# Block sums of the down projection's weights loaded into their own place, and output rows with buffers of their own, in a one-core encoder layer

## The chip, the cores and the metric

The kernel runs on one core of a Trainium2 chip (trn2). The metric is the device time of one execution in microseconds (us), the median over several runs. The profiled execution is one run of its own; its trace has a span (first instruction to last) a little shorter than its time.

## The reference

One layer of an encoder over 512 positions of 1024 features, all in float32: a norm, a combined projection, gated spatial mixing beside dilated window attention, a merge, and then a feed-forward block. The change lies in the last two lines of it:

```python
n2 = rms_norm(h, norm_mlp_pre[l])
hid = jnp.square(jax.nn.relu(jnp.einsum('bsd,df->bsf', n2, w_up[l])))     # 512 x 4096
mlp_out = jnp.einsum('bsf,fd->bsd', hid, w_down[l])                       # 512 x 1024
h = h + rms_norm(mlp_out, norm_mlp_post[l])
```

## The kernel before

**Products in three parts.** TensorE (PE) multiplies float32 values as pairs: `split_into` (L78 to L80) has ScalarE (ACT) write the high part and VectorE (DVE) write the low part, source minus high part. A product is three matmuls, high by high, high by low, low by high (`acc3`, L1026 to L1030). A split weight piece is called `hl` and has 5 buffers; a split piece of the hidden activations is called `hhl`. One split is 128x1024 elements on ACT and as many on DVE.

**The up projection** (loop at L970) runs in 14 rounds. The last round's results leave the accumulators by ACT L983, L986, L988 and DVE L984, L990, L992, L993, and last of all by DVE L998, after which ACT applies Relu (L1000) and Square (L1001). L998 is the last reader of one accumulator bank.

**The down projection** sums over 4096 hidden features, that is 32 tiles of 128. The first 16 tiles are done in eight plain steps (`plain`, two tiles each, 48 matmuls of 128x512). The other 16 are done as two chunks `c` of a 2-by-2 block scheme with seven products of block sums in place of eight (Winograd's form): `first_sums` forms b22 - b12 into `tsum[c]` and sums of the hidden blocks into `a21` and `s2`; later steps add b11 to `tsum`, subtract it from b22, and subtract it from b21. Weight loads go through a tag `raw` with two buffers of 1 MB (names `dnw`), issued by SyncE's queue (SP). A load waits until both what the buffer held is split or summed, and SP waits in order, so a load that has to wait holds the ones behind it.

**The order.** Each engine takes its instructions strictly in the order in which the scheduler of the language left them; the scheduler places an instruction by its own estimate of when it is ready. In that order three plain steps come first, then `first_sums(0)`, plain step 3, `first_sums(1)`, plain step 4, and the products of the block sums with three more plain steps between. Loads of `first_sums` use the same two `raw` buffers: b22 and b12 of a chunk fill both, and the next plain step's weights wait until the two subtractions (L1079) have read them.

**The end.** The last 24 matmuls finish output rows 0 and 1 (tiles of 128 positions); rows 2 and 3 were finished by the 24 before. `finish` (L1139) loads the residual `h2` for the row (queue of GpSimd, POOL), squares the row on ACT with its output as junk into `o` (L1154), multiplies by the gain on DVE (L1155, `y`), forms the norm's factor (DVE L93, then POOL L96), writes `o` (L1149, two halves) and sends it out (L1151, two DMAs of 256 KB from SP). `o` has two buffers (`lpool`), so row 0 takes the buffer of row 2 and row 1 that of row 3.

**Buffers.** `n2pool` has 8 places of 512 KB under the tag `n2`. In the up projection they hold the moving operand of the matmuls; afterwards they take `gain3`, `s2` (two), `v`, `t1` (four), and `h2` (four). `tsum` has 2 MB of its own (`sumpool`).

Of the kernel before, what the change touches and what calls it, by code (L numbers as in the profile page):

```python
# [10 lines left out]
F32 = mybir.dt.float32  # L11
F32R = mybir.dt.float32r
AF = mybir.ActivationFunctionType
ALU = mybir.AluOpType
PSUM = bass.MemoryType.PSUM

P = 128
S = 512
D = 1024
# [17 lines left out]
def block_kernel(ctx: ExitStack, tc: tile.TileContext, x, norm_mix_pre, w_in, b_gate, ln_v_gain, ln_v_bias,  # L37
                 w_spatial, b_spatial, w_branch_a, w_branch_b, w_out, norm_mix_post, norm_mlp_pre, w_up,
                 w_down, norm_mlp_post, ident_c, rope_c, mask_c, perm_c, out):
    nc = tc.nc  # L40
    x, out, w_in, w_up, w_down, w_out = x[0], out[0], w_in[0], w_up[0], w_down[0], w_out[0]
    w_branch_a, w_branch_b, w_spatial = w_branch_a[0], w_branch_b[0], w_spatial[0]

    def pool(stack, name, bufs=1, space=None, side=None):
        kw = {"side": side} if side else {}
        if space is not None:
            kw["space"] = space
        return stack.enter_context(tc.tile_pool(name=name, bufs=bufs, reuse_waits="tile", **kw))
# [20 lines left out]
    def wsplit(raw, pl=None, bufs=None, tag="w", sub=None):  # L69
        pl = pl or wpool  # L70
        shape = list(raw.shape)
        hi = pl.tile(shape, F32R, name="hi", tag=tag + "hi", bufs=bufs)
        lo = pl.tile(shape, F32R, name="lo", tag=tag + "lo", bufs=bufs)
        nc.scalar.activation(hi, raw, AF.Copy)  # L74
        (sub or nc.vector).tensor_tensor(lo, raw, hi.bitcast(F32), op=ALU.subtract)  # L75
        return hi, lo
# [210 lines left out]
    def feature_tile(wh, wl, nk, mh, ml, tag="acc"):  # L287
        ps = psA.tile([P, S], F32, name="pf", tag=tag, bufs={"acc": 4, "S": 2, "T": 1, "y": 1}[tag])
        for k in range(nk):
            mm3(ps, (wh[:, k], wl[:, k]), (mh[:, k], ml[:, k]), k == 0, k == nk - 1)  # L290
        return ps
# [27 lines left out]
    for i, (vec, n) in enumerate(((b_gate, 16), (ln_v_gain, 4), (ln_v_bias, 4), (norm_mlp_pre, 8))):  # L319
        o = (0, 16, 20, 24)[i]  # L320
# [24 lines left out]
    def seven_pairs(n, weights, moving, banks, snap, two, rows, evac, after):  # L345
        tail = None
        for i in range(n):
            c2, c1 = rows(i)
            w = weights(i)
            Y, Z, X = banks()  # L350
            product(6, Y, w, moving, True)
            if tail:
                tail()
            product(1, X, w, moving, True)
            p1, z5, u2, u3 = snap("p1", two), snap("z5", 1), snap("u2", 1), snap("u3", 1)
            nc.scalar.activation(p1, X, AF.Copy)
            nc.vector.tensor_tensor(u2, Y, p1, op=ALU.add)
            product(5, Z, w, moving, True)
            nc.scalar.activation(z5, Z, AF.Copy)
            product(2, X, w, moving, False)  # L360
            evac(i, c1[:, A], X)
            product(7, Y, w, moving, False)
            nc.vector.scalar_tensor_tensor(u3, Y, -1.0, p1, op0=ALU.mult, op1=ALU.subtract)
            product(3, Z, w, moving, False)
            nc.vector.tensor_tensor(c1[:, B], Z, u2, op=ALU.add)
            nc.vector.tensor_tensor(c2[:, B], u3, z5, op=ALU.subtract)

            def tail(i=i, w=w, Y=Y, p1=p1, c2=c2):
                product(4, Y, w, moving, False)
                nc.vector.scalar_tensor_tensor(c2[:, A], Y, -1.0, p1, op0=ALU.mult, op1=ALU.subtract)  # L370
                after(i)
        tail()
# [312 lines left out]
    for g2 in range(2):  # L685
        raw = wload([KD, 2 * P], lambda r: [(r, fcols(w_in, COL_U + g2 * 2 * P, KD, 2 * P))], "uw")
        for j in range(2):
            g = 2 * g2 + j
            wh, wl = wsplit(raw[:, :, j * P:(j + 1) * P], sub=nc.gpsimd)
            ps = psA.tile([P, S], F32, name="pf", tag="acc" if g else "T", bufs=4 if g else 1)  # L690
# [74 lines left out]
    for d in range(GSTD):  # L765
        g2 = gate_rows(d - GSTD)
        raw = gate_raw(d)
        for br in range(2):
            ps = feature_tile(*wsplit(raw[:, :, 1 - br]), KD, nhn, nln)
# [11 lines left out]
    n2pool = pool(back, "n2pool", bufs=8, side="right")  # L781
# [9 lines left out]
    halves = [slice(0, 512), slice(512, 1024)]  # L791
# [171 lines left out]
    def half_bank(tag):  # L963
        return psB.tile([P, 512], F32, name="p" + tag, tag=tag, bufs=4)[:, :256]
# [5 lines left out]
    for i in range(NSTD, KF // 2):  # L970
# [6 lines left out]
        Y, Z, X = half_bank("acc"), half_bank("acc"), half_bank("tp")  # L977
# [28 lines left out]
    lpool = pool(dn, "lpool", bufs=2)  # L1006
# [4 lines left out]
    X, W, Y, Z = [[accs[t][hf] for t in ts] for ts, hf in (((0, 1), 0), ((0, 1), 1), ((2, 3), 0), ((2, 3), 1))]  # L1011
# [5 lines left out]
    def raw_down():  # L1017
        return wback.tile([P, 2, D], F32, name="dnw", tag="raw", bufs=2)
# [7 lines left out]
    def acc3(ps, a, b, start, stop):  # L1026
        (ah, al), (bh, bl) = a, b
        nc.tensor.matmul(ps, ah, bh, start=start, stop=False, skip_group_check=True)  # L1028
        nc.tensor.matmul(ps, ah, bl, start=False, stop=False, skip_group_check=True)  # L1029
        return nc.tensor.matmul(ps, al, bh, start=False, stop=stop, skip_group_check=True)  # L1030
# [12 lines left out]
    w7 = w_down[F7 * P:].rearrange("(c j h p) d -> c h p j d", p=P, h=2, j=4)  # L1043

    def block(c, h, hf):
        raw = raw_down()
        raw = raw.rearrange("p a (b d) -> p (a b) d", d=512)
        nc.sync.dma_start(raw, w7[c, h, :, :, halves[hf]])
        return raw
# [23 lines left out]
    tsum = sumpool.tile([P, N7, 512], F32, name="tsum")  # L1073
    tsum = [tsum[:, 4 * c:4 * c + 4] for c in range(2)]
    s2 = []

    def two(out, x, y, op):
        for i in range(0, 4, 2):
            nc.vector.tensor_tensor(out[:, i:i + 2], x[:, i:i + 2], y[:, i:i + 2], op=op)  # L1079

    def first_sums(c):
        b22, b12 = block(c, 1, 1), block(c, 0, 1)
        two(tsum[c], b22, b12, ALU.subtract)
        nc.vector.tensor_tensor(a21[c], a11[c], a21[c], op=ALU.subtract)
        s2.append(n2pool.tile([P, 4, 256], F32, name="s2", tag="n2"))
        nc.vector.tensor_tensor(s2[c], a22[c], a21[c], op=ALU.subtract)

    first_sums(0)
    plain(3, order)
    first_sums(1)  # L1090
    plain(4, y_first)
    keep = hida.tile([P, 8, S], F32, name="hid")
# [34 lines left out]
    for c in range(2):  # L1127
        b22 = block(c, 1, 1)
# [10 lines left out]
    def finish(t, srcs, ys, o, ss):  # L1139
        h2 = n2pool.tile([P, D], F32, name="h2", tag="n2")  # L1140
        nc.gpsimd.dma_start(h2, h2d[tsl[t]])
        for hf in (1, 0):
            if srcs[hf] is not None:
                if ys[hf] is None:
                    ys[hf] = lpool.tile([P, 512], F32, name="y")
                weigh(srcs[hf], ys[hf], o[:, halves[hf]], ss, hf)
        r = rstd_of(ss, 1.0 / D)
        for hf, hs in enumerate(halves):
            nc.vector.scalar_tensor_tensor(o[:, hs], ys[hf], r, h2[:, hs], op0=ALU.mult, op1=ALU.add)  # L1149
        for hs in halves:  # L1150
            nc.sync.dma_start(out[tsl[t], hs], o[:, hs])  # L1151
# [23 lines left out]
    for ps, (hh, hl), ws, ts in ((Y, h4, w4, (2, 3)), (X, h, w, (0, 1))):  # L1175
        for t in range(2):
            for j in range(4):
                wh, wl = ws[j // 2]
                acc3(ps[t], (hh[:, j, tsl[t]], hl[:, j, tsl[t]]), (wh[:, j % 2], wl[:, j % 2]), False, j == 3)
            o = lpool.tile([P, D], F32, name="o")  # L1180
            if ps is Y:
                nc.vector.tensor_tensor(p1[:, t], Y[t], p1[:, t], op=ALU.add)
                finish(2 + t, [p1[:, t], None], [p1[:, t], r22[:, t]], o, sums[2 + t])
            else:
                finish(t, [X[t], None], [None, r12[:, t]], o, sums[t])
# [43 lines left out]
```

## Time and profile before

| What | Value |
|---|---|
| median of 3 runs | 803.08 us (802.73 to 803.18) |
| profiled execution, its own time | 802.89 us |
| its span | 801.1 us |
| TensorE matmul busy | 782.8 us, 98% of the span |
| VectorE busy | 593.8 us, 74% |
| ScalarE busy | 442.1 us, 55% |
| GpSimd busy | 60.2 us, 8% |
| mean granted TensorE clock | 0.995 |
| last matmul begins | 790.01 us |

The page of a profile gives busy times, a picture of the span in 40 slices, the DMA queues, the chain of work that ended last, the costliest groups and the DMA issues. A timeline row reads: start, length, engine, line of the code, operation, output and input names (buffer numbers left out), shape, count, and in brackets the idle time before it with what ended it. Matmul rows overlap: their starts are what counts, some 0.227 us apart when PE never waits. A row of the waits view reads: engine and line that waited, what it waited for, us in total, times, longest. A DMA's time to landing runs from its issue to the signal that its data are there.

### The profile page before, as it was taken

Reading aid. Unit: us, or ns where it says so; the run is one execution under the profiler, and the core shown is the slowest. Engines: PE = TensorE matmul, PEld = TensorE weight load, DVE = VectorE, ACT = ScalarE, POOL = GpSimd, SP = SyncE. Lnnn points to the kernel's source line nnn. Section 1 sums busy time; section 2 is a strip of 40 time slices with the busy share of each in tenths; the row PEclk is TensorE's granted clock in tenths of the full one; section 3 lists DMA queues with packets and bytes.
Section 4 is the critical chain, followed back from the end, with each engine's and each line's share of the span. In section 5 each row is a group of like instructions: output and inputs, shape, how many; then the busy total and the mean of one; then the engine's idle time right before and its main releaser. Section 6 shows DMA issues by size and latency. Waiting matters only on the chain.

```text
span 801.1 us, 12250 instructions
## 1 busy us (share of the span) xinstructions
PE 782.8 (98%) x4869; PEld 709.8 (89%) x4869; DVE 593.8 (74%) x956; ACT 442.1 (55%) x731; POOL 60.2 (8%) x86
## 2 busy tenths in 40 slices
PE   9999999999999999999999999999999999999994
PEld 6899999998988889999988899999999887888883
DVE  6784678978654878788646479988888546896686
ACT  6351467978576454455435447666667424543551
POOL 3300100010104300000001102000000000000001
PEclk9999999999999999999999999999999999999997
DMA  9733733353615423253456222433333354143302
GB/s 310 232 122 100 203 102 106 96 142 94 190 62 135 140 79 107 79 142 95 132 184 197 93 79 66 145 106 106 106 106 123 114 206 162 64 147 131 132 1 105
DMA packets 93706, 101.01 MB, mean 126 GB/s; under 512 B 2721, under 2 KB 74433, under 8 KB 93650
## 3 DMA queue, kind: packets, MB, share of 16 engines
q1 hardware_dynamic: 83312, 79.70, 32.0%
q0 software_dynamic: 10336, 20.54, 8.4%
q8 instruction: 38, 0.62, 0.3%
q14 instruction: 18, 0.15, 0.1%
q10 hardware_dynamic: 2, 0.00, 0.0%
HBM read 90.27 MB, written 9.96 MB: 125 GB/s over the span
## 4 chain that ended last, share of the span: by engine, by line
PE 87%; DVE 5%; DMA 3%; ACT 3%; issue 1%; POOL 0%; DVEq 0%; POOLq 0%; ACTq 0%
PE pacc L961 12%; PE pg L343 9%; PE pgacc L343 6%; PE pd L1028 5%; PE pf L84 5%; PE pd L1029 5%; PE pd L1030 5%; PE pf L85 5%; PE pf L86 5%; PE ptp L961 5%; PE pv L85 4%; PE pv L86 4%; PE pv L84 4%; PE pgS L343 3%; DMA dnw<-in_w_down_dram 2%; PE pd L84 2%
## 5 line engine op out<-in xcount | busy, mean ns | idle before, releaser
L1029 PE MATMUL pd<-hl,hhl 128*128 128x512 f32 x240 | 93.3, 389 | 0.0
L1030 PE MATMUL pd<-hl,hhl 128*128 128x512 f32 x240 | 91.3, 389 | 0.0
L1028 PE MATMUL pd<-hl,hhl 128*128 128x512 f32 x240 | 88.7, 390 | 1.4 <-ACT hl L79 1.4
L961 PE MATMUL pacc<-nt,hl 128*128 128x256 f32 x504 | 66.7, 279 | 1.4 <-DVE nt L80 1.4
L961 PEld LDWEIGHTS pacc<-nt,hl 128*128 128x128 f32 x504 | 62.2, 188 | 1.6 <-DVE nt L80 1.6
L1028 PEld LDWEIGHTS pd<-hl,hhl 128*128 128x128 f32 x240 | 45.0, 188 | 11.1 <-ACT hl L79 1.9
L1030 PEld LDWEIGHTS pd<-hl,hhl 128*128 128x128 f32 x240 | 45.1, 188 | 9.3
L1029 PEld LDWEIGHTS pd<-hl,hhl 128*128 128x128 f32 x240 | 45.1, 188 | 9.3
L79 ACT ACTIVATE hl<-dnw 128x1024 fp32r<-128x1024 f32 x28 | 29.3, 1055 | 40.6 <-PE pd L1030 17.1
L80 DVE TENSOR_TENSOR hl<-dnw,hl 128x1024 fp32r<-128x1024 f32 x28 | 33.9, 1221 | 15.9 <-ACT hl L79 15.9
L961 PE MATMUL pacc<-n,hl 128*128 128x256 f32 x336 | 44.7, 279 | 0.0
L74 ACT ACTIVATE hi<-s 128x1024 fp32r<-128x1024 f32 x30 | 31.7, 1059 | 23.6 <-DVE s L330 8.3
L84 PE MATMUL pf<-nh,hi 128*128 128x512 f32 x112 | 44.6, 398 | 0.0
L85 PE MATMUL pf<-nl,hi 128*128 128x512 f32 x112 | 43.9, 392 | 0.0
L86 PE MATMUL pf<-nh,lo 128*128 128x512 f32 x112 | 43.9, 392 | 0.0
L75 DVE TENSOR_TENSOR lo<-s,hi 128x1024 fp32r<-128x1024 f32 x30 | 36.6, 1224 | 9.7 <-ACT hi L74 9.6
L961 PEld LDWEIGHTS pacc<-n,hl 128*128 128x128 f32 x336 | 41.7, 188 | 0.1
L79 ACT ACTIVATE hl<-s 128x1024 fp32r<-128x1024 f32 x28 | 29.6, 1056 | 21.8 <-DVE s L945 15.5
L80 DVE TENSOR_TENSOR hl<-s,hl 128x1024 fp32r<-128x1024 f32 x28 | 34.2, 1221 | 6.2 <-ACT hl L79 6.2
L85 PE MATMUL pv<-lo,nh 128*128 128x512 f32 x96 | 38.2, 397 | 0.0
L86 PE MATMUL pv<-hi,nl 128*128 128x512 f32 x96 | 37.8, 397 | 0.0
L84 PE MATMUL pv<-hi,nh 128*128 128x512 f32 x96 | 37.1, 395 | 0.0
(387 smaller groups left out, 2223.4 us busy)
## 6 DMA issues: line engine op xcount, KB each, us to landing
dnw<-in_w_down_dram SPq DMA_DIRECT2D x18, 1024.0 KB, 4.9
upw<-in_w_up_dram SPq DMA_DIRECT2D x16, 1024.0 KB, 5.6
qkw<-in_w_in_dram SPq DMA_DIRECT2D x24, 512.0 KB, 5.1
gw<-in_w_in_dram SPq DMA_DIRECT2D x16, 512.0 KB, 5.2
slab<-in_w_in_dram SPq DMA_DIRECT2D x6, 1024.0 KB, 9.1
wow<-in_w_out_dram SPq DMA_DIRECT2D x4, 1024.0 KB, 4.9
w0raw<-in_w_in_dram SPq DMA_DIRECT2D x4, 512.0 KB, 6.8
v0d<-v POOLq DMA_DIRECT2D x4, 512.0 KB, 4.7
```

What stands on the lines that cost most here:

```text
L74: nc.scalar.activation(hi, raw, AF.Copy)
L75: (sub or nc.vector).tensor_tensor(lo, raw, hi.bitcast(F32), op=ALU.subtract)
L79: nc.scalar.activation(hi, src, AF.Copy)
L80: return sub.tensor_tensor(lo, src, hi.bitcast(F32), op=ALU.subtract)
L84: nc.tensor.matmul(ps, ah, bh, start=start, stop=False)
L85: nc.tensor.matmul(ps, ah, bl, start=False, stop=False)
L86: return nc.tensor.matmul(ps, al, bh, start=False, stop=stop)
L343: nc.tensor.matmul(ps, a[:, j], b[:, j], start=first and not (j or i), stop=(j == KH - 1 and i == 2), skip_group_check=True)
L961: nc.tensor.matmul(ps, a[:, j], b[:, j], start=first and not (j or m), stop=(j == KH - 1 and m == 2), skip_group_check=True)
L1028: nc.tensor.matmul(ps, ah, bh, start=start, stop=False, skip_group_check=True)
L1029: nc.tensor.matmul(ps, ah, bl, start=False, stop=False, skip_group_check=True)
L1030: return nc.tensor.matmul(ps, al, bh, start=False, stop=stop, skip_group_check=True)
```

## The change

`first_sums` no longer goes through the two `raw` buffers. b12 is loaded straight into `tsum[c]` (1 MB, one DMA), b22 in two halves of 512 KB, each into a spare place of `n2pool` (tile `b22`), and each half is subtracted in place (new L1085). `two` becomes one instruction of 128x2048 elements in place of two of 128x1024; its remaining uses are the additions of b11 and the subtractions from b21. The last two rows' `o` are taken from `n2pool` (name `o2`), each with a place of its own.

```diff
     def two(out, x, y, op):
+        nc.vector.tensor_tensor(out, x, y, op=op)
+
+    def first_sums(c):
+        nc.sync.dma_start(tsum[c], w7[c, 0, :, :, halves[1]])
         for i in range(0, 4, 2):
-            nc.vector.tensor_tensor(out[:, i:i + 2], x[:, i:i + 2], y[:, i:i + 2], op=op)
-
-    def first_sums(c):
-        b22, b12 = block(c, 1, 1), block(c, 0, 1)
-        two(tsum[c], b22, b12, ALU.subtract)
+            b22 = n2pool.tile([P, 2, 512], F32, name="b22", tag="n2")
+            nc.sync.dma_start(b22, w7[c, 1, :, i:i + 2, halves[1]])
+            nc.vector.tensor_tensor(tsum[c][:, i:i + 2], b22, tsum[c][:, i:i + 2], op=ALU.subtract)
...
-            o = lpool.tile([P, D], F32, name="o")
+            o = lpool.tile([P, D], F32, name="o") if ps is Y else n2pool.tile([P, D], F32, name="o2", tag="n2")
```

The scheduler moves instructions with it. On SP's queue, from the first load for the down projection on (with `b_7075` and `b_7078` the halves of b22 for chunk 0, `b_7144` and `b_7147` those for chunk 1):

```order
-L1035 DMA dnw<-in_w_down_dram 128x2x1024 x3
-L1048 DMA dnw<-in_w_down_dram 128x4x512 x2
+L1035 DMA dnw<-in_w_down_dram 128x2x1024 x2
+L1084 DMA b_7075<-in_w_down_dram 128x2x512
 L1035 DMA dnw<-in_w_down_dram 128x2x1024
-L1048 DMA dnw<-in_w_down_dram 128x4x512 x2
-L1035 DMA dnw<-in_w_down_dram 128x2x1024
+L1084 DMA b_7078<-in_w_down_dram 128x2x512
+L1081 DMA tsum<-in_w_down_dram 128x4x512 x2
+L1084 DMA b_7144<-in_w_down_dram 128x2x512
+L1084 DMA b_7147<-in_w_down_dram 128x2x512
+L1035 DMA dnw<-in_w_down_dram 128x2x1024 x2
```

All loads of both `first_sums` now stand together, between the loads of plain step 2 and plain step 3; the loads of plain steps 3 and 4 stand behind them in a row. In the built program `b_7075` waits for PE's product 1 of the last up round, `b_7078` and with it both `tsum` loads for its product 2, `b_7144` and `b_7147` for its product 3, for these read the places that the loads fill. The load of plain step 3 waits for the last low part of plain step 1's weights, that of plain step 4 for the last one of plain step 2's.

On DVE at the end of the up projection (L998 is the last evacuation of the last up round; the `hl` ahead of it belong to plain step 1, the first one behind it to plain step 2), a piece of the difference:

```order
 L80 TENSOR_TENSOR hl<-dnw,hl 128x1024
+L1085 TENSOR_TENSOR tsum<-b_7075,tsum 128x1024
+L1085 TENSOR_TENSOR tsum<-b_7078,tsum 128x1024
 L998 SCALAR_TENSOR_TENSOR hid<-pacc,p_6800 128x256
 L80 TENSOR_TENSOR hl<-dnw,hl 128x1024
-L80 TENSOR_TENSOR hhl<-hid,hhl 128x1024 x3
-L1084 TENSOR_TENSOR hid<-hid 128x4x256
-L80 TENSOR_TENSOR hl<-dnw,hl 128x1024
-L1086 TENSOR_TENSOR s_7149<-hid 128x1024
-L1079 TENSOR_TENSOR tsum<-dnw 128x1024 x2
-L80 TENSOR_TENSOR hhl<-hid,hhl 128x1024
+L1085 TENSOR_TENSOR tsum<-b_7144,tsum 128x1024
```

The two subtractions of chunk 0 now stand ahead of L998, the first one of chunk 1 ahead of the low part of plain step 1's activations (the first of the three `hhl`), and the second one, the next `+` row but one, behind that of plain step 2's. Before, chunk 0's stood eight instructions behind L998 and chunk 1's further still.

On POOL at the end of the program, before (`h_7882`, `h_7910`, `h_7937`, `h_7965` are the residuals of rows 2, 3, 0 and 1, `rs_out` the norm's factors in the same order of rows):

```order
L1141 DMA h_7882<-h2d 128x1024
L1141 DMA h_7910<-h2d 128x1024
L1141 DMA h_7937<-h2d 128x1024
L1141 DMA h_7965<-h2d 128x1024
L96 TENSOR_TENSOR rs_out<-rs_in_7888,neghalf 128x1
L96 TENSOR_TENSOR rs_out<-rs_in_7916,neghalf 128x1
```

and now, with the rows in the same order and row 1's residual as `h_7963`:

```order
L1143 DMA h_7880<-h2d 128x1024
L1143 DMA h_7908<-h2d 128x1024
L1143 DMA h_7935<-h2d 128x1024
L96 TENSOR_TENSOR rs_out<-rs_in_7886,neghalf 128x1
L96 TENSOR_TENSOR rs_out<-rs_in_7914,neghalf 128x1
L1143 DMA h_7963<-h2d 128x1024
L96 TENSOR_TENSOR rs_out<-rs_in_7942,neghalf 128x1
```

The residual of row 1 is now loaded after the factors of rows 2 and 3, where all four loads stood ahead of all factors before. On DVE at the end, the gain products and sums of squares of rows 0 and 1 (L1157 and L93 in the new numbering) now stand one after the other ahead of both rows' outputs (L1151); before, row 0's outputs stood between them. PE's order is the same up to plain step 3; from there on it differs only in whether the high and low parts of a weight piece are used in turn or the high part first, with the same 720 matmuls of 128x512 in the down projection.

## The prediction

> **What bounds the kernel now.** I read the page first, then the busy time by stretches of the second feed-forward half.
>
> ```profile
> span 801.1 us, 12250 instructions
> PE 782.8 (98%) x4869; PEld 709.8 (89%) x4869; DVE 593.8 (74%) x956; ACT 442.1 (55%) x731; POOL 60.2 (8%) x86
> 668.00:673.00 5.00, 3.56 (x16) 2.60 (x15) 2.64 (x3) 3.73 (x4) 0.00 (x0) 1.00 0.69 266
> 673.00:785.00 112.00, 112.00 (x495) 92.72 (x495) 88.91 (x88) 55.55 (x65) 2.17 (x4) 1.00 0.27 94
> 791.00:801.00 10.00, 0.00 (x0) 0.00 (x0) 4.25 (x8) 1.38 (x4) 1.10 (x2) 0.59 0.43 162
> ```
>
> The last three rows give a stretch, its length, the busy time of PE, weight load, DVE, ACT and POOL, then granted clock, DMA share and GB/s. PE is the bound almost everywhere; in 112 us from 673 on it never rests. Only two places are to be had: a hole of 1.44 us near 669 and the 10 us behind the last matmul. A part of the change falls on each. The chain of waits says how the hole comes about (start, length, what):
>
> ```profile
> 646.43 2.37 DVE tsum L1079 x2
> 648.82 4.75 DMA dnw<-in_w_down_dram
> 657.07 4.87 DMA dnw<-in_w_down_dram
> 662.04 2.37 DVE tsum L1079 x2
> 664.43 4.82 DMA dnw<-in_w_down_dram
> 669.27 1.06 ACT hl L79
> ```
>
> No PE row stands in it: load, sum, load, sum, load follow each other through the two raw buffers, and the last load, plain step 4's, ends in PE's wait. The timeline of PE around it, with the same place one step earlier for comparison:
>
> ```profile
> 657.67 0.39 PE L1030 MATMUL pd<-hl,hhl 128*128 128x512 f32 x1
> 657.89 1.98 PE L1028 MATMUL pd<-hl,hhl 128*128 128x512 f32 x8
> 659.71 0.39 PE L1029 MATMUL pd<-hl,hhl 128*128 128x512 f32 x1
> ...
> 668.55 0.39 PE L1030 MATMUL pd<-hl,hhl 128*128 128x512 f32 x1
> 670.38 2.14 PE L1028 MATMUL pd<-hl,hhl 128*128 128x512 f32 x8 [1.44 <-ACT hl L79]
> 672.36 0.39 PE L1029 MATMUL pd<-hl,hhl 128*128 128x512 f32 x1
> ```
>
> Undisturbed, the step from one L1030 over eight matmuls to the next L1029 takes 659.71 - 657.67 = 2.04 us; here it takes 672.36 - 668.55 = 3.81. So the hole costs 1.77 us: the start is 1.60 late, and 0.17 goes in the first eight matmuls behind it.
>
> The end, from the timelines of PE, DVE, ACT and POOL:
>
> ```profile
> 790.01 0.39 PE L1030 MATMUL pd<-hl,hhl 128*128 128x512 f32 x1
> 788.08 2.74 DVE L1149 SCALAR_TENSOR_TENSOR o<-hid,rs_out,h 128x512 f32<-128x512 f32 x4 [0.39 <-POOL rs_out L96]
> 791.72 0.60 ACT L1154 ACTIVATE o<-pd 128x512 f32<-128x512 f32 x1 [4.82 <-DMA out_dram<-o]
> 792.44 0.69 DVE L1155 TENSOR_TENSOR y<-pd,gain 128x512 f32<-128x512 f32 x1 [1.62 <-ACT o L1154]
> 793.05 0.15 DVE L93 SCALAR_TENSOR_TENSOR rs_in<-ss,rs_in 128x1 f32<-128x1 f32 x1
> 793.34 0.55 POOL L96 TENSOR_TENSOR rs_out<-rs_in,neghalf 128x1 f32<-128x1 f32 x1 [4.78 <-DVE rs_in L93]
> 793.93 0.75 DVE L1149 SCALAR_TENSOR_TENSOR o<-y,rs_out,h 128x512 f32<-128x512 f32 x1 [0.73 <-POOL rs_out L96]
> 797.41 0.75 DVE L1149 SCALAR_TENSOR_TENSOR o<-hid,rs_out,h 128x512 f32<-128x512 f32 x1
> ```
>
> ACT could square row 0 as soon as its matmuls are done. It waits 4.82 us until row 2's output has left the buffer that it writes its junk into, and DVE behind it 1.62.
>
> **The sum.** The profiled execution took 802.89 us, its span 801.1; the other 1.79 stays. It lies 0.02% under the median of 803.08, so the terms are taken from 802.89.
>
> *The hole near 669 goes: -1.77.* Plain step 3's load now waits only for the last low part of plain step 1's weights, and plain step 4's for that of plain step 2's. These two rows of DVE, and a third that is needed just below:
>
> ```profile
> 629.63 1.23 DVE L80 TENSOR_TENSOR hl<-dnw,hl 128x1024 fp32r<-128x1024 f32 x1 [0.67 <-ACT hl L79]
> 640.22 1.22 DVE L80 TENSOR_TENSOR hl<-dnw,hl 128x1024 fp32r<-128x1024 f32 x1
> 676.04 1.22 DVE L80 TENSOR_TENSOR hhl<-hid,hhl 128x1024 fp32r<-128x1024 f32 x1
> ```
>
> So the loads start at some 631 and 641, the second a few us later for the subtractions that now stand ahead, and both land some 10 us or more before PE asks (657.9 and 668.8). The loads after them move up in the same way, and splits from there on wait for PE to free an `hl` buffer, as they do from 673 on today without a rest for PE; next late is then nothing until the end. The one subtraction or addition of 2048 elements in place of two of 1024 is not in the trace; two take 2.37, one should take 2.2 to 2.5, and it lies beside the same gapless PE: 0. It makes a low part of activations behind it wait 1.2 longer, covered: the split ran at 676.04, and its product stands 72 matmuls behind 670.38, at 0.227 each near 686.7.
>
> *A new wait at the start of plain step 1.* The subtractions of chunk 0 stand ahead of L998, and they wait for a load that can't start before product 2 of the last round. What stands there now:
>
> ```profile
> 625.73 0.39 ACT L988 ACTIVATE hid<-ptp 128x256 f32<-128x256 f32 x1 [3.54 <-PE ptp L961]
> 632.68 0.42 DVE L998 SCALAR_TENSOR_TENSOR hid<-pacc,p 128x256 f32<-128x256 f32 x1 [1.82 <-PE pacc L961]
> 633.65 1.04 ACT L1000 ACTIVATE hid<-hid 128x1024 f32<-128x1024 f32 x1
> 634.59 2.94 ACT L79 ACTIVATE hhl<-hid 128x1024 fp32r<-128x1024 f32 x3
> 634.77 0.39 PE L1028 MATMUL pd<-hl,hhl 128*128 128x512 f32 x1
> 636.13 0.39 PE L1028 MATMUL pd<-hl,hhl 128*128 128x512 f32 x1
> 639.76 1.98 PE L1030 MATMUL pd<-hl,hhl 128*128 128x512 f32 x8
> ```
>
> Product 2 is over by 625.7 (ACT's first row waits for it). The second half of b22 (0.5 MB) and then `tsum[0]` (1 MB) start there. How long that takes, from the SP timeline and the group of these loads:
>
> ```profile
> 649.24 8.20 SPq L1048 DMA_DIRECT2D dnw<-in_w_down_dram  x2
> DMA to landing us min/median/max: 4.7/4.9/7.1
> ```
>
> Alone, 1 MB takes 4.75 (the chain's load of 648.82, landed at 653.57). The load issued at 649.24 behind it took up to 7.1, to 656.34: 2.77 for one more MB in line. So 1.5 MB takes 4.75 + 1.39 = 6.14 and lands at 631.9; ahead of it, three loads (0.5 MB for b22, 0.5 for the gain, 1 for plain step 2) are to be through by 625.7, which leaves little room, so I take 632.2, with 631.3 and 633 as ends. The two subtractions take 2.3 until the next instruction begins, so L998 starts at 634.5 in place of 632.68 and ends at 634.95; Relu follows on ACT, 0.94 later the high part of the activations (633.65 to 634.59), and 1.11 behind its start PE can use it (669.27 to 670.38): 637.0. PE asks at 636.13. That is 0.87 late, and with the 0.17 of a restart **+1.0**; nothing if the load lands by 631.3, 1.8 if at 633. The bank that L998 frees is asked for at 634.77, 0.2 before its new end, and that wait lies within the other. Behind L998 on DVE, the first subtraction of chunk 1 needs 3 MB through: 4.75 + 2 x 2.77 = 10.3, at 636.0; the low part of the activations behind it is then written by 638.5, and PE asks at 639.76. That cover of 1.3 us is thin; beyond it PE loses one for one.
>
> One rule speaks to this term. The Trainium skill, "DMA: Bandwidth & Descriptors", section "Anatomy of one DMA", puts a transfer at about 2.0 us plus its bytes by 436 GB/s; an estimate from it for 1.5 MB is 5.6 us, a landing at 631.3, and with it a sum of 798.1. The rows are slower for 1 MB (4.75 against 4.4 by that rule), so they decide.
>
> *The end: -3.0.* With its own buffer row 0, whose last matmul stands five ahead of the last, is squared near 789.4, and row 1 once the last matmul is through at 790.4, done at 791.05. DVE is busy with rows 2 and 3 until 788.08 + 2.74 = 790.8 and becomes the limit. Then y for row 0 at 790.8, its sum 0.6 later (792.44 to 793.05) at 791.4, y for row 1 at 791.6, its sum at 792.2. A sum's factor is ready for DVE 0.88 after it (793.05 to 793.93): 792.3 and 793.1. Row 0's outputs start at 792.35 and 793.0 (0.67 each, 2.74 by four), row 1's at 793.7 and 794.4, in place of 797.41. What follows the last output stays. Spare places for `o2` cost nothing: they hold sums and splits read long before.
>
> Sum: 802.89 - 1.77 + 1.0 - 3.0 = **799.1**.
>
> **The rivals.** *No new wait:* the first `tsum` lands by 631.3. For it, half of b22 is loaded earlier and the median landing is near the minimum; against it, 1.5 MB in line after a crowded queue. 798.1.
>
> *Row 1's residual is late.* Its load now stands on POOL behind the factors of rows 2 and 3.
>
> ```profile
> 786.96 1.61 POOL L96 TENSOR_TENSOR rs_out<-rs_in,neghalf 128x1 f32<-128x1 f32 x2 [36.89 <-DVE rs_in L93]
> DMA to landing us min/median/max: 2.9/3.5/6.3
> ```
>
> The second row is the group of the `h` loads and stores. Issued at 788.57, it lands at 791.5, 792.1 or, at worst, 794.9, while four output writes leave; it is needed at 793.7. At worst the end is 1.2 later: 800.3. The same page, section "Queues, rings and completion order", says each DMA engine takes turns between queues, so the load would share with those writes and not stand behind them; no row here shows the two together.
>
> *Both `tsum` loads come in together* rather than one by one: 2.5 MB, 4.75 + 1.5 x 2.77 = 8.9, at 634.6. PE then waits 3.3 + 0.17 = 3.5: 801.6. Against it: the load of 648.82 landed as fast as one alone with another in line behind it.
>
> *Slower than before:* DVE stands on the subtraction so long that L998, Relu and all splits behind it starve PE. It decides once the first `tsum` lands later than 631.3 + 4.6 = 635.9, for then the new wait eats 1.77 + 3.0. If all that is queued shares the engines (2.5 MB, 1 MB for chunk 1's b22, 1 for plain step 3), it is 4.5 MB: 4.75 + 3.5 x 2.77 = 14.4, at 640.1, a wait of 9.0: 807.1. The same row speaks against it.
>
> *The change doesn't do what it says near 669:* another wait, of an `hl` buffer or of ACT, holds plain step 4 as long. Then 1.77 stays: 800.9. Against it: ACT began that split at 669.27, 0.02 behind the load's landing (664.43 + 4.82).
>
> **How the numbers follow.** Forecast 0.50; no new wait 0.20; late residual 0.15; both loads together 0.08; starved PE 0.03; hole stays 0.04. The low end is no new wait and 0.2 more at the end, 797.9; the high end takes in the late residual with the load landing at 633 (800.3 + 0.8), 801.1. What lies outside is the 0.11 of the cases above and a little below. The bound of 0.2%, about what a measurement of this kernel tells from no change, is 1.6 us: faster is under 801.5, slower over 804.7. Faster: all cases but starving and half of both-together, 0.93; within it 0.04; slower 0.03.
>
> **What would show it.** In the profile after: PE without a hole near 669; a wait of DVE L1085 for `tsum`'s load, then PE's L1028 waiting for ACT L79 `hhl` near 636, some 0.9 us; no ACT wait for an output DMA; y of rows 0 and 1 in a row, and the last output 3 us closer to the last matmul. Wrong: a PE wait over 2 us near 636, a wait of L1151 for the `h` load, or a hole elsewhere between 640 and 785.

## The result, and the profile after

The changed kernel takes 801.07 us (median of 11 runs, 800.79 to 802.54), the kernel before beside it 803.15; the ratio is 0.9975, with a 95% interval of 0.9967 to 0.9984. So it is faster by 2.0 us, half of the 4.0 that were forecast. Two executions are used nowhere, one of an experiment (the first profiled one of e6 below, 2764.78 us, so that e6's stretches come from a second one, e6b) and one of before beside the last experiments (1578.76 us).

The profiled execution of after took 801.01 us. The first two lines of its page:

```profile
span 799.2 us, 12243 instructions
PE 782.9 (98%) x4869; PEld 709.5 (89%) x4869; DVE 593.7 (74%) x952; ACT 442.4 (55%) x731; POOL 60.6 (8%) x86
```

PE is busy as long as before, and the span is 1.9 us shorter. To see where, I cut the end of the program into three stretches by rows that every kernel here has. **A** goes from the start of the last up product on PE (a group of twelve L961 near 631, whose result L998 reads) to the start of the last matmul, **B** from there to the start of the last pass that writes an output, **C** from there to the end of the span. PE does the same work ahead of A in all kernels; from execution to execution A's start differs by up to 1.3 us, so the stretches are compared and not the points of time. The rows of before that the prediction does not show:

```profile
631.08 1.56 PE L961 MATMUL pacc<-n,hl 128*128 128x256 f32 x12
634.55 0.39 PE L1030 MATMUL pd<-hl,hhl 128*128 128x512 f32 x1
```

and those of after, with PE's two waits between them and DVE at the end:

```profile
631.24 1.56 PE L961 MATMUL pacc<-n,hl 128*128 128x256 f32 x12
634.71 0.39 PE L1030 MATMUL pd<-hl,hhl 128*128 128x512 f32 x1
635.96 0.50 PE L1028 MATMUL pd<-hl,hhl 128*128 128x512 f32 x1 [0.87 <-DVE hid L998]
638.06 0.50 PE L1028 MATMUL pd<-hl,hhl 128*128 128x512 f32 x1 [0.45 <-ACT hhl L79]
641.83 1.98 PE L1030 MATMUL pd<-hl,hhl 128*128 128x512 f32 x8
668.00:671.00 3.00, 3.00 (x15) 2.49 (x14) 2.25 (x1) 0.00 (x0) 0.00 (x0) 1.00 0.00 0
790.29 0.39 PE L1030 MATMUL pd<-hl,hhl 128*128 128x512 f32 x1
791.02 0.69 DVE L1157 TENSOR_TENSOR y<-pd,gain 128x512 f32<-128x512 f32 x1
791.68 0.69 DVE L1157 TENSOR_TENSOR y<-pd,gain 128x512 f32<-128x512 f32 x1
794.51 0.75 DVE L1151 SCALAR_TENSOR_TENSOR o<-hid,rs_out,h 128x512 f32<-128x512 f32 x1
```

- A: 790.01 - 631.08 = 158.93 before, 790.29 - 631.24 = 159.05 after. The hole near 669 is gone (PE is busy for all of 668 to 671), and two new waits take back what it gave: from the L1030 ahead of them to the group of eight L1030 it was 639.76 - 634.55 = 5.21, now 641.83 - 634.71 = 7.12.
- B: 797.41 - 790.01 = 7.40 before, 794.51 - 790.29 = 4.22 after. This is the gain of 3.2.
- C: 801.1 - 797.41 = 3.69 before, 799.2 - 794.51 = 4.69 after. This is a loss of 1.0 that I had at nothing. (Spans are printed to 0.1 us, so each C is good to 0.05.)

With the 0.16 that A starts later, 0.12 - 3.18 + 1.00 + 0.16 = -1.90, the difference of the spans.

Why the two waits come, from the timelines of SP, DVE and ACT in after:

```profile
626.19 1.01 SPq L1081 DMA_DIRECT2D tsum<-in_w_down_dram  x2
633.21 2.36 DVE L1085 TENSOR_TENSOR tsum<-b,tsum 128x1024 f32<-128x1024 f32 x2 [2.19 <-DMA tsum<-in_w_down_dram]
635.49 0.42 DVE L998 SCALAR_TENSOR_TENSOR hid<-pacc,p 128x256 f32<-128x256 f32 x1
636.00 1.06 ACT L1000 ACTIVATE hid<-hid 128x1024 f32<-128x1024 f32 x1 [2.10 <-DVE hid L998]
636.97 2.94 ACT L79 ACTIVATE hhl<-hid 128x1024 fp32r<-128x1024 f32 x3
```

The first `tsum` block lands at 633.1, DVE subtracts for 2.3 us, and only then comes L998, which both frees a bank (PE's first wait) and feeds Relu and the split of plain step 1's activations (PE's second wait).

The prediction counted 1.5 MB up to that landing. What SP's queue moved between the issue of the second half of `b22` (625.77) and the landing (packets, MB of a million bytes, share of 16 engines):

```profile
q1 hardware_dynamic: 1165, 2.32, 88.3%
```

In this unit the half of `b22` and the first `tsum` are 1.57 MB; some 0.7 MB more had been moved by then, nearly all for loads that were issued behind them. By 631.36 the queue had moved 1.62 MB, 1.8 us ahead of the landing. For the load of 648.82 in before, from which the price was taken, 1.27 MB had been moved when its 1.05 landed, with one load behind it; here four were issued behind. So loads in line on one queue are not moved strictly one after the other. That this overlap alone makes the landing late is read from the bytes; no run tries it.

For the end, the output writes and what else is under way. First before, then after: SP's issues, the writes' time from issue to landing, and in after POOL's load of row 1's residual:

```profile
788.86 9.65 SPq L1151 DMA_DIRECT2D out_dram<-o  x8
DMA to landing us min/median/max: 2.0/2.1/2.1
```

```profile
789.14 6.48 SPq L1153 DMA_DIRECT2D out_dram<-o  x8
DMA to landing us min/median/max: 2.6/4.2/4.3
788.81 0.58 POOL L1143 DMA_DIRECT2D h<-h2d  x1
h<-h2d POOLq DMA_DIRECT2D x1, 512.0 KB, 4.5
```

The four writes of rows 2 and 3 take 4.2 to 4.3 us instead of 2.1, those of rows 0 and 1, which set the end, 2.6 to 2.7 instead of 2.0. How the engines were shared in one microsecond of that (the DMA view of after, 791.5 to 792.5; packets, MB, share of 16 engines):

```profile
q0 software_dynamic: 63, 0.26, 70.2%
q1 hardware_dynamic: 58, 0.12, 30.5%
```

q0 is the load, q1 the writes: nearly as many packets of one as of the other, and as the load's hold about 4 KB (0.26 MB in 63) and the writes' about 2 KB (0.12 in 58), two thirds of the bytes are the load's. The Trainium skill, "DMA: Bandwidth & Descriptors", section "Queues, rings and completion order", says that each DMA engine takes turns between the queues it has work for; the trace agrees with its 63 and 58 packets. In which order one engine took them it does not tell.

### The profile page after: what moved, and what is told of

Same layout as the page of the kernel before. It is cut to its first block, busy times and chain, and to the rows that moved or that the text cites. A ratio compares the mean times of both kernels' runs of the same rounds, so it can differ in the third digit from the quotient of the medians.

```text
span 799.2 us, 12243 instructions
## 1 busy us (share of the span) xinstructions
PE 782.9 (98%) x4869; PEld 709.5 (89%) x4869; DVE 593.7 (74%) x952; ACT 442.4 (55%) x731; POOL 60.6 (8%) x86
## 4 chain that ended last, share of the span: by engine, by line
PE 91%; DVE 4%; ACT 2%; DMA 1%; issue 1%; POOL 0%; DVEq 0%; SPq 0%; POOLq 0%; ACTq 0%
PE pacc L961 11%; PE pg L343 9%; PE pd L1028 6%; PE pd L1029 6%; PE pd L1030 6%; PE pgacc L343 6%; PE pf L84 5%; PE pf L85 5%; PE pf L86 5%; PE ptp L961 5%; PE pv L85 4%; PE pv L86 4%; PE pv L84 4%; PE pgS L343 3%; PE pd L84 2%; PE pd L86 2%
## 5 line engine op out<-in xcount | busy, mean ns | idle before, releaser
L1029 PE MATMUL pd<-hl,hhl 128*128 128x512 f32 x240 | 93.3, 389 | 0.0
L1028 PE MATMUL pd<-hl,hhl 128*128 128x512 f32 x240 | 91.8, 390 | 1.3 <-DVE hid L998 0.9
L1030 PE MATMUL pd<-hl,hhl 128*128 128x512 f32 x240 | 91.1, 389 | 0.0
L961 PE MATMUL pacc<-nt,hl 128*128 128x256 f32 x504 | 66.7, 279 | 1.4 <-DVE nt L80 1.4
L961 PEld LDWEIGHTS pacc<-nt,hl 128*128 128x128 f32 x504 | 62.2, 188 | 1.6 <-DVE nt L80 1.6
L1030 PEld LDWEIGHTS pd<-hl,hhl 128*128 128x128 f32 x240 | 45.1, 188 | 9.3
L961 PE MATMUL pacc<-n,hl 128*128 128x256 f32 x336 | 44.7, 279 | 0.0
L961 PEld LDWEIGHTS pacc<-n,hl 128*128 128x128 f32 x336 | 41.7, 188 | 0.1
```

The costliest lines, as they stand in the source:

```text
L961: nc.tensor.matmul(ps, a[:, j], b[:, j], start=first and not (j or m), stop=(j == KH - 1 and m == 2), skip_group_check=True)
```

## The experiments

Three theories. *A:* row 1's residual, loaded beside the output writes, makes C longer by 1.0; rival: the eight writes, 0.67 us apart now, are too close by themselves. *B:* the subtractions ahead of L998 make both waits near 636; rival: PE would be late there anyway. *C*, SP's closing waits, came after the first runs. All kernels with their stretches, each worked out as above from that kernel's own rows (ratio to the kernel before on the same chip):

| kernel | median us | ratio (95%) | A | B | C | landing of writes |
|---|---|---|---|---|---|---|
| before | 803.15 | | 158.93 | 7.40 | 3.69 | 2.0/2.1/2.1 |
| after | 801.07 | 0.9975 (0.9967, 0.9984) | 159.05 | 4.22 | 4.69 | 2.6/4.2/4.3 |
| e1 outputs only | 802.84 | 0.9978 (0.9967, 0.9989) | 161.01 | 4.16 | 4.65 | 2.9/3.0/4.4 |
| e2 sums only | 803.23 | 0.9988 (0.9979, 0.9997) | 159.07 | 6.77 | 4.16 | 2.0/2.1/2.1 |
| e3 residual early | 801.38 | 0.9960 (0.9946, 0.9973) | 159.49 | 3.80 | 4.19 | 2.1/2.1/2.1 |
| e4 sums behind | 799.24 | 0.9936 (0.9925, 0.9948) | 157.14 | 4.23 | 4.79 | 2.7/4.2/4.4 |
| e5 both | 798.96 | 0.9929 (0.9913, 0.9944) | 157.14 | 3.81 | 4.16 | 2.1/2.1/2.1 |
| e6 behind L998 only | 799.51 | 0.9939 (0.9922, 0.9955) | 157.14 | 4.23 | 4.90 | 2.8/4.4/4.5 |
| e7 residual twice | 804.20 | 0.9995 (0.9984, 1.0006) | 159.10 | 4.21 | 7.21 | 4.4/5.2/6.8 |
| e8 residual in halves | 802.87 | 0.9978 (0.9966, 0.9990) | 159.07 | 4.45 | 5.56 | 3.5/3.8/5.3 |
| e9 both, and closing | 798.34 | 0.9921 (0.9902, 0.9940) | 157.15 | 3.81 | 3.75 | 2.1/2.1/2.7 |
| e10 before, two more loads | 806.25 | 1.0013 (0.9999, 1.0027) | 159.50 | 7.37 | 4.58 | 2.0/2.1/2.1 |

The kernel before was slower beside the experiments (medians 803.74, 804.61 and 804.41) than beside after (803.15), so ratios came out lower than forecast in several of them. The readings therefore rest on the stretches.

**One part alone: the output buffers (e1).**

```
 # in the kernel before
-            o = lpool.tile([P, D], F32, name="o")
+            o = lpool.tile([P, D], F32, name="o") if ps is Y else n2pool.tile([P, D], F32, name="o2", tag="n2")
```

> The kernel before with one of the two edits, the last two rows' own output buffers. Theory A (row 1's residual load is now in the way of the output writes): the stretch from the last matmul to the start of the last combining pass falls from 7.40 to about 4.2 us, the stretch from there to the end of the span grows from 3.69 to about 4.7 us, the last writes take over 4 us from issue to landing; 3.18 - 1.0 = 2.2 us faster than before, ratio 0.9973. If what follows the last output stays as it was, as predicted: 3.2 us faster, ratio 0.9960.

B and C are as theory A had them (4.16 and 4.65), and so is the ratio. But the last writes take 2.9 to 3.0 us, not over 4, and A is 2.1 longer than before, with the hole left in. The wait of PE and the stretches around it, from the timeline and the windows (last three columns: granted clock, that is the share of its full clock that TensorE was given, DMA share, GB/s):

```profile
671.36 3.42 PE L1028 MATMUL pd<-hl,hhl 128*128 128x512 f32 x8 [1.92 <-ACT hl L79]
668.42:671.83 3.41, 1.49 (x7) 0.94 (x6) 0.49 (x1) 1.58 (x2) 0.00 (x0) 1.00 1.02 405
671.83:675.24 3.41, 3.41 (x10) 2.63 (x9) 3.41 (x4) 3.41 (x5) 0.00 (x0) 0.50 0.27 79
675.24:678.65 3.41, 3.41 (x16) 2.77 (x16) 3.41 (x4) 0.81 (x1) 0.00 (x0) 1.00 0.78 279
```

The hole was 0.48 longer than before's 1.44, and behind it the granted clock was 0.50 for 3.41 us, so that eight matmuls took 3.42 us instead of 2.14. In before the clock behind the hole was 1.00. Half of 3.41 is 1.7, and with the 0.48 that is near the 2.08 that A grew. So the hole can cost more than its length. The twelve runs of e1 lie between 800.87 and 803.96, the median at a ratio that fits the forecast; the low end would be runs without the fall of the clock, which is argued and not shown. The load of row 1's residual goes with this part of the edit: it was issued at 791.11 in e1, and at 750.3 in e2.

**The other part alone: the block sums (e2).**

```
 # in the changed kernel
-            o = lpool.tile([P, D], F32, name="o") if ps is Y else n2pool.tile([P, D], F32, name="o2", tag="n2")
+            o = lpool.tile([P, D], F32, name="o")
```

> The changed kernel with the other edit alone, the block sums in their own place and spare buffers; all four output rows share two buffers as before. Theory B (the subtractions in front of L998 wait for the first sum block's load and hold PE): the hole near 669 is gone (-1.77 us), PE waits near 636 come (+1.91 us), the end is as before; the time is that of before within 0.4 us, ratio 1.000. By the prediction's own price of the wait (+1.0) it would be 0.8 us faster, ratio 0.999.

The profile is as theory B had it: no hole, the same two waits as after (0.85 and 0.44 us), A 159.07, within 0.14 of before; A, B and C together are 170.00 us against 170.02. The block sums alone give nothing. The ratio of the times, 0.9988, fits the prediction's own price better; the kernel before is slower in many executions than in its profiled one, and the last section says what that may come from. B is 0.63 shorter, which no theory named: row 2's first output was issued 790.57 - 788.95 = 1.62 ahead of the last matmul instead of 790.01 - 788.86 = 1.15, and row 0's square waits for it; DVE's waits for the factors of rows 0 and 1 were 0.66 instead of 0.73. C is 0.47 longer, though the writes land in 2.0 to 2.1 us; theory C, below, has the reason.

**Near 636: the subtractions held back (e4, e6).** In e4 behind the low part of plain step 2's activations, in e6 behind L998 alone; the orders on PE and SP are those of after.

```
 # e4; e6 has last_bank[0], which tail() sets to L998's instruction, in place of last_split[2]
-            split_into(hl[:, 0], hl[:, 1], src)
+            last_split.append(split_into(hl[:, 0], hl[:, 1], src))
...
-            nc.vector.tensor_tensor(tsum[c][:, i:i + 2], b22, tsum[c][:, i:i + 2], op=ALU.subtract)
+            with tc.issue_after(last_split[2].ins): nc.vector.tensor_tensor(tsum[c][:, i:i + 2], b22, tsum[c][:, i:i + 2], op=ALU.subtract)
```

> The changed kernel with its four subtractions held behind the split of the last plain step's hidden tile on the vector engine; order on PE and SP unchanged. Theory B: L998 starts near 632.8 again, both PE waits near 636 go, 1.9 us faster than the changed kernel: 799.2 us, ratio to before 0.9951. Rival (PE would be late there anyway, by the loads in front of the hidden split or by more work on the vector engine): at most the 0.87 us of the bank wait goes, 800.2 us or more, and a PE wait stays between 636 and 650.

> The changed kernel with the subtractions held behind L998 alone, so that they still stand in front of the low half of the hidden tile's split on the vector engine. If L998's place alone makes both PE waits (the second one by way of the Relu and the copy that follow it on the scalar engine): both go, 799.2 us, as with the subtractions behind everything. If the second wait comes from the split that stands behind the subtractions: only about 1.0 us goes, 800.1 us, and a PE wait for hhl stays near 638.

> The same kernel as in the run with the subtractions behind L998 alone, for its profile near 636. If L998's place alone makes both PE waits: none there, the last matmul about 1.5 to 1.9 us earlier against L998's start than in the changed kernel. If the second comes from the split behind the subtractions: a PE wait for hhl near 638.

DVE in e4:

```profile
633.24 0.42 DVE L998 SCALAR_TENSOR_TENSOR hid<-pacc,p 128x256 f32<-128x256 f32 x1 [1.82 <-PE pacc L961]
634.33 1.23 DVE L80 TENSOR_TENSOR hl<-dnw,hl 128x1024 fp32r<-128x1024 f32 x1 [0.67 <-ACT hl L79]
636.23 2.36 DVE L80 TENSOR_TENSOR hhl<-hid,hhl 128x1024 fp32r<-128x1024 f32 x2 [0.67 <-ACT hhl L79]
638.51 1.22 DVE L1085 TENSOR_TENSOR tsum<-b,tsum 128x1024 f32<-128x1024 f32 x1
```

and in e6:

```profile
633.53 0.42 DVE L998 SCALAR_TENSOR_TENSOR hid<-pacc,p 128x256 f32<-128x256 f32 x1 [1.83 <-PE pacc L961]
633.98 2.36 DVE L1085 TENSOR_TENSOR tsum<-b,tsum 128x1024 f32<-128x1024 f32 x2
636.26 1.22 DVE L80 TENSOR_TENSOR hl<-dnw,hl 128x1024 fp32r<-128x1024 f32 x1
637.39 1.22 DVE L80 TENSOR_TENSOR hhl<-hid,hhl 128x1024 fp32r<-128x1024 f32 x1
```

In neither does PE wait between 630 and 788, and A is 157.14 in both: 1.91 less than after, 1.79 less than before. Theory B holds, and L998's place alone is what counts; the loads in front and the added work on DVE cost PE nothing. In e6 the low part of plain step 1's activations is still behind two subtractions (637.39) and in time.

**The end: the residual loads (e3, e7, e8).** In e3 all four are issued ahead of the last block loop; in e7 row 1's is loaded a second time into a spare buffer that nobody reads; in e8 each is cut into two halves.

```
 # e3
-        h2 = n2pool.tile([P, D], F32, name="h2", tag="n2")
-        nc.gpsimd.dma_start(h2, h2d[tsl[t]])
+        h2 = h2s[t]
...
+    h2s = {t: n2pool.tile([P, D], F32, name="h2", tag="n2") for t in (2, 3, 0, 1)}
+    for t in (2, 3, 0, 1):
+        nc.gpsimd.dma_start(h2s[t], h2d[tsl[t]])
     for c in range(2):
         b21 = block(c, 1, 0)
 # e7
-        nc.gpsimd.dma_start(h2, h2d[tsl[t]])
+        for to in [h2] + [n2pool.tile([P, D], F32, name="again", tag="n2") for _ in range(t == 1)]: nc.gpsimd.dma_start(to, h2d[tsl[t]])
 # e8
-        nc.gpsimd.dma_start(h2, h2d[tsl[t]])
+        for hs in halves: nc.gpsimd.dma_start(h2[:, hs], h2d[tsl[t], hs])
```

> The changed kernel with all four residual loads issued ahead of the last block loop instead of one in each row's finish, so that none is under way beside the output writes. Theory A: the writes land 2.1 us after their issue again, the stretch from the last combining pass to the end of the span is 3.7 us again, 1.0 us faster than the changed kernel: 800.1 us, ratio to before 0.9963. Rival (eight writes of 256 KB at 0.67 us apart are too close for the DMA engines by themselves): landing stays at about 4 us and the time at 801.1.

> The changed kernel with row 1's residual loaded twice, the second time into a spare buffer that nobody reads. Theory A (the writes lose the bytes that the load takes from the same engines): another 0.5 MB, that cost 1.0 us the first time, makes the end later by 0.8 to 1.4 us: 801.9 to 802.5 us, ratio 0.9985 to 0.9992, and the writes take over 4.3 us to land. Rival (the writes are too close by themselves): 801.1 us.

> The changed kernel with each residual loaded in two halves with rows of 2 KB, as the writes have, instead of one with rows of 4 KB; bytes and time of issue as in the changed kernel. If only the sum of the bytes counts, since load and writes use the same engines and these are never idle in between: 801.1 us within 0.2, though the first writes land earlier and the load later. If the writes lose because the other queue's descriptors are twice as long: they land about 0.5 us earlier and the time is 800.6.

e3's writes, at the same 0.67 us from one to the next:

```profile
789.98 6.54 SPq L1153 DMA_DIRECT2D out_dram<-o  x8
DMA to landing us min/median/max: 2.1/2.1/2.1
```

They land in 2.1 us again, so the rival falls: the writes by themselves are not too close. But C went down to 4.19 only, not to 3.7, so theory A is half of it. A is 0.44 longer than in after, for the first `tsum` landed that much later against A's start (DVE's subtraction began at 634.53 - 632.12 = 2.41 behind it instead of 633.21 - 631.24 = 1.97). B fell by another 0.4, unforeseen: POOL's factors of rows 2 and 3 ran singly (0.56 and 1.00 us) instead of as one group of 1.60, and the outputs began earlier; why, I did not follow.

e7 shows the load's price from the other side, and it is higher than forecast: C 7.21, 2.5 more than after where 0.8 to 1.4 was expected. The DMA view from 790 to 796, after and then e7:

```profile
DMA packets 997, 2.09 MB, mean 349 GB/s; under 512 B 103, under 2 KB 103, under 8 KB 997
q0 software_dynamic: 144, 0.52, 32.0%
```

```profile
DMA packets 666, 1.75 MB, mean 292 GB/s; under 512 B 66, under 2 KB 66, under 8 KB 666
q0 software_dynamic: 286, 1.04, 63.2%
q1 hardware_dynamic: 380, 0.71, 30.5%
```

With two loads in the way less is moved in all (1.75 MB in 6 us against 2.09): the writes lose more than the bytes of the load.

e8 does not do what it was made for. Its queue q0, in the same stretch:

```profile
q0 software_dynamic: 160, 0.52, 30.9%
```

After has 144 such packets for the same 0.52 MB (above). The 16 more are small ones that close a second transfer; the data still goes in packets of 4 KB. So the length of the load's packets is not tried, and both expectations fail: two transfers in place of one made C 0.87 longer.

**What is left of C: SP's closing waits (e10, e9).** At the program's end SP tests the completion semaphores of its transfers one after the other; there are eight, used in turn, and each test is a row like these of after:

```profile
L1227 SPq EVENT_SEMAPHORE  x11: 17/28/28, 795.7 to 799.2; - x11
SPq L1227 <- DMA out_dram<-o: 2.2, 2, 1.6
```

The change puts two transfers more on SP's queue, and with that the last output moves from the eighth of the eight semaphores to the second. The starts of SP's records at the end, us:

```
kernel             last write issued   its completion seen   tests behind it   first drain   span end
before                  798.18              800.22                 0              800.30       801.1
after                   795.29              797.95                 6              798.41       799.2
e1 outputs only         797.52              800.46                 0              800.54       801.4
e2 sums only            798.11              800.15                 6              800.62       801.5
e5 both                 794.12              796.20                 6              796.67       797.5
e9 both, and closing    793.22              795.32                 0              795.39       796.2
e10                     798.9               800.94                 6              801.70       802.7
```

In after the six tests behind start 0.06 us apart although all that they ask for is long done, 0.46 us from the completion to the drain instead of 0.08. So C's 1.00 is 2.66 - 2.04 = 0.62 for the landing and 0.38 for these tests. That is theory C. e1 and e2 show the two parts by themselves. In e2, with the two more transfers and no load beside the writes, the last write lands as in before (2.04) and the drain comes 0.47 behind it. In e1, with the load and without the two transfers, no test stands behind, and the last write alone takes 2.94, 0.90 more than before. So e1 met theory A's 4.7 by luck: the load's part was larger there (0.90) than in after (0.62), and the tests' part was missing. e10 gives the kernel before two transfers more, far from the end; e9 takes two away from e5, by writing rows 2 and 3 with one transfer each:

```
 # e10, in the kernel before: block() issues n transfers, and b11 is loaded with n = 2
-        nc.sync.dma_start(raw, w7[c, h, :, :, halves[hf]])
+        for i in range(0, 4, 4 // n): nc.sync.dma_start(raw[:, i:i + 4 // n], w7[c, h, :, i:i + 4 // n, halves[hf]])
 # e9, in e5 (e3 and e4 together)
-        for hs in halves:
+        for hs in halves if t < 2 else [slice(0, D)]:
```

> The changed kernel with both repairs, the residual loads issued early and the subtractions held back. If theories A and B are both right the gains add, since one lies at 636 and the other behind the last matmul: 801.1 - 1.0 - 1.9 = 798.2 us, ratio to before 0.9938. If only B is right 799.2, if only A 800.1.

> The kernel before with two of its block loads, far ahead of the end, cut into two transfers each and nothing else changed, so that the last output's completion is the second of the eight that SP tests at the end. Theory C: the writes land 2.0 to 2.1 us after their issue as before, but from the last data to the end of the span it takes 1.65 us instead of 1.25, 0.4 us more: 803.4 us, ratio 1.0005 (less than the times can tell, so the profile's closing rows decide). Rival: 1.25 us, 803.1.

> The kernel with both repairs, and rows 2 and 3 written with one transfer each instead of two, so that SP's queue has two transfers fewer and the last output's completion is the last of the eight that SP tests at the end of the program, instead of the second. Theory C (what is left of the longer end is SP's closing waits: six of them stand behind the one that the last output releases, at 0.06 us each): last data to the end of the span 1.25 us instead of 1.66, 0.4 us faster than with both repairs alone: 798.5 us, ratio 0.9924. Rival (the end behind the last data differs for another reason): 1.66 us stays, 798.9 us.

e5 has both repairs in its stretches (A as in e4, B and C as in e3): 165.11 in all, 2.85 less than after's 167.96 where 2.9 was forecast, but 0.41 of that is B's and only 0.53 C's. Its time is 0.3 under e4's, which these runs don't tell apart, and 0.8 over the 798.2 forecast. e9 follows theory C: with the last output on the eighth semaphore, completion to drain takes 0.07 instead of 0.47, and C is 3.75, 0.41 less than e5's. Its interval (0.9902 to 0.9940) lies clear of after's; its median, 798.34 us, is the lowest of the study, though not told apart from e5's. e10 has the six tests too (800.94 to 801.33), with its writes at 2.0 to 2.1 as before; but the drain behind the last test began 0.37 us after it instead of 0.07, for which I have no reason, and its hole near 669 was 2.02 us, so C (4.58) and the time came out higher than expected.

## Why the prediction was half wrong, step by step

- *The hole near 669 goes, -1.77.* Right: A without the new wait (e4) is 157.14 against 158.93, -1.79. Nothing came in its place up to the end.
- *A new wait, +1.0.* Right in its mechanism, wrong in its size: 159.05 - 157.14 = 1.91. The term that failed is the landing of the first `tsum`: taken at 632.2, measured 633.1 (DVE starts at 633.2), a little above the upper end of 633 for which 1.8 was given. The sum priced 1.5 MB in line, with what is issued behind costing nothing; 2.32 MB instead of 1.57 (in the view's unit) had been moved when it landed. The fit that the prediction sets beside this term stands in the Trainium skill, "DMA: Bandwidth & Descriptors", section "Anatomy of one DMA", for transfers that GpSimd issues; these loads were SP's, so its landing at 631.3 was no estimate for them. From there on the steps held: two subtractions of 2.28, Relu and split by 636.97, PE 1.09 later. The wait for the bank came first and was seen by PE, but it lies within the other as said, since the sum is set by `hhl`. Each of the two restarts ran a first matmul of 0.50 us instead of 0.39.
- *The end, -3.0.* Right: B is 3.18 shorter, with y and outputs in the order that was worked out.
- *"What follows the last output stays."* Wrong, and the larger of the two misses: +1.00. The step that failed is that the writes were given the landing time of before, with nothing beside them. The prediction had looked at row 1's residual as something that might come too late for its reader. It came in time (landed at 793.3, read from 793.85 on); the ones it held up were the output writes. That is 0.62 of it in this execution (0.90 in e1). The other 0.38 is SP's closing tests, moved by nothing but the count of transfers.
- The rest is A's later start (0.16 here) and 0.18 more gain at the end.

Of the rivals, *no new wait* asked for a landing at 631.3 and fell to the same row; *row 1's residual is late* had the right transfer and the wrong victim; *both loads together* fell as stated, since the first landed at 633.1, not at 634.6, and the second 2.7 later, but it had the direction right: loads behind the first did move beside it; no PE wait was left near 669 and PE did not starve.

## What to carry to other kernels

A transfer that is moved is to be priced by what it runs beside as well as by whether it arrives in time: here 0.5 MB on another queue doubled the landing time of four writes (4.2 us instead of 2.1) and made the last one, which sets the end, 0.6 to 0.9 us later, though the load's reader never waited. A load's landing is to be priced with the loads issued behind it, too. An instruction that waits for a load must not be let in front of one on the same engine that releases PE; here one line that holds it back was worth 1.9 us, nearly as much as the whole edit gained. What follows the last instruction is part of the sum too: find out which completion the program's end tests last.

## What was not expected of the hardware

- With two DMA queues at work, the packets they got were nearly the same in number (63 to 58 in one microsecond), so the queue with 4 KB packets took twice the bytes of the one with 2 KB packets.
- Loads in line on one queue overlap: 2.32 MB had been moved when the first 1.57 landed, with four loads issued behind.
- Each semaphore test at the end costs SP 0.06 us even where there is nothing to wait for; six of them 0.38 us.
- An idle time of 1.92 us on PE was followed in one execution by a granted clock of 0.50 for 3.41 us (e1). The Trainium skill, "TensorE: Matmul & The Clock Gate", section "Part 1: The HAM clock gate (the "warmup" mystery)", lets the clock fall after an idle window of about 3.4 us; here it fell after a stretch of that length in which PE was idle for 1.92 us only, while the holes of 1.44 (before) and 2.02 (e10) left it at 1.00. Where a hole lies seems to decide. The clock's changes in e1 are whole multiples of 3.413 us apart (671.83, 675.24 and, behind the last matmul, 798.12). Laid out in such steps back from the last fall, the twelve profiled executions agree from the clock's first rise (10 to 14 us) on: each stretch with PE busy for 1.49 us or less was followed by 0.50 (e1's hole, and the end of every kernel), each with 1.68 or more by 1.00. e1's hole lies in one stretch (1.49 busy); e10's is split between two (1.89 and 2.91), and so is before's (2.46 and 2.92). Only e1 has such a fall ahead of the end, and no run shifts a hole to try it.
- The kernel before, which has this hole, spreads from 803.11 to 806.53 us on the chip of e1 and e2, e2 without it from 803.0 to 804.33. Of the executions of before beside all experiments, 13 of the 14 between 805.9 and 807.2 us have a mean granted clock of 0.993 or 0.994 (one 0.995), the 30 under 804 one of 0.995 to 0.997; 3.41 us at 0.50 lower that mean by 0.002. So a lower clock goes with the longer times; that it falls behind this hole there is likely and not shown.
